# Residual in chunk stacks at the norms between the layers' halves, normed in place by wide operations

## The chip, the cores and the metric

One core of a Trainium2 chip runs the whole kernel. The metric is the device time in microseconds (us); lower is better. TensorE does the matrix products; VectorE, ScalarE and GpSimd do elementwise work on tiles in SBUF (VectorE and ScalarE also in PSUM, where the products land); SP issues nearly all transfers. In the profile they are PE, DVE, ACT, POOL and SP.

## What is computed

One inference step of a two-layer decoder trunk in fp32: 1024 prompt tokens and 8 decoded tokens, width 1024, hidden width 2816. Layer 0 mixes with a gated linear recurrence (HGRN2), layer 1 with sliding-window attention on keys and values that are projected once, after layer 0. Every sub-layer adds a gated result to the residual stream `h`, and reads it through an RMS norm with a scale and a shift that come from the conditioning vector (adaLN):

```python
def rms_norm(x, g):
    y = x32 * lax.rsqrt(jnp.mean(x32 * x32, axis=-1, keepdims=True) + EPS)
    return y * g.astype(jnp.float32)
def modulate(x, g, shift, scale):
    return rms_norm(x, g) * (1.0 + scale[:, None, :]) + shift[:, None, :]
...
        h = h + g1[:, None, :] * mix                      # mix = mixer(xn) @ w_o
        xn = modulate(h, norm_w[l, 1], sh2, sc2)
        h = h + g2[:, None, :] * swiglu(xn, w_ffn_in[l], w_ffn_out[l])
        if l == N_A_LAYERS - 1:
            kvn = modulate(h, kv_norm_w, sh_kv, sc_kv)
            k_sh, v_sh = jnp.split(kvn @ w_kv, 2, axis=-1)
```

## The kernel before

**Layout.** Activations lie transposed: features on the 128 partitions (8 tiles, `k` from 0 to 7), the 1032 tokens as columns, the last 8 of them decoded. Two grids cut the columns: `G3` in three chunks of 344 and `G4` in four of 258. The residual is `h[k]`, a tile of 1024 columns for each `k`, with the decoded tokens in `hd`.

**Products.** Each fp32 factor is split in a high and a low part, and `mm3` (L283 to L285) makes three matmuls per block: high x high, high x low, low x high. Weights arrive as raw tiles (SP), ScalarE rounds the high part (L182), and GpSimd subtracts to get the low part (L185, tile `wu`).

**Around the change.** After a mixer its output is multiplied by the output weights in two halves of the contraction: `wo_first` on `G3` (beside the recurrence or the attention of the other heads), `wo_second` on `G4`. Each 128-row block `n` of a chunk takes 12 matmuls (`wo_product`) and ends in `residual` (L718; L722 for the decoded tokens), which adds the gated product to `h`. For each chunk `wo_second` then runs a norm: squares (ScalarE L649, L652) and their sums (L654, on VectorE and GpSimd in turn), the two sums joined (L666), column sums by TensorE (L672), the inverse root by Newton steps of small VectorE operations (L677, L542 to L551), a diagonal matrix of it (L680, "the diagonal" below), a matmul that spreads it over the partitions (L689), a copy to SBUF (L690). `apply_steps` then does three narrow operations per `k`: `h` times scale and norm (VectorE L698), plus the shift, rounded to the high part (ScalarE L702), and the low part (VectorE L703). These steps are generators in the list `later`, of which `step()` advances one at a time between the blocks of the product.

The result feeds the gated product of the feed-forward part, which multiplies 2 x 2 blocks by seven products instead of four times two; `factors` makes the seven right factors from the *split* values, by wide VectorE operations over four `k` (L1255 to L1257 for a difference, L1249 on ScalarE and L1250 on VectorE to split it). `prepare_all` stores `h` to DRAM first (L1294), and `back` loads it again for the second feed-forward product. There the sum of squares (`ToKV` for layer 0) runs in the same way on `G3`; `ToKV` is applied twice, once for keys and values and once for the queries of layer 1. `conditioning` (L472, 128x32 matmuls on the adaLN weights, which SP loads at L276) runs beside `wo_first` and `wo_second` of layer 0.

**The order.** The program is written as these interleaved generators; when the kernel is built, a scheduler fixes the sequence of each engine's instructions, and semaphores tie them. A change of what is written moves rows on every queue. SP's queue is in order too: a store that waits for its data holds the loads behind it.

## Time and profile before

| | |
|---|---|
| median of 3 runs | 2569.52 us (2567.04 to 2572.01) |
| profiled execution, its own time | 2565.16 us |
| its span, first to last instruction | 2563.4 us |
| mean granted TensorE clock | 0.987 |
| busy: TensorE, VectorE, ScalarE, GpSimd | 97%, 56%, 33%, 31% |
| moved by DMA | 293.42 MB, 114 GB/s |

The span is one profiled execution. In timelines the first number is the start in us from the start of the span, the second the busy time, and what stands in square brackets is idle time just before and what ended it. In lists of waits, "A <- B: 6.8, 1, 6.8" says that A's engine sat idle 6.8 us until B let A go, once. The granted clock is a share of full speed.

### The profile page before, as it was taken

The page shows a single profiled execution, that of the slowest core. Times are in us where ns is not written, and L with a number is a line of the kernel's source. Part 1 is how long each engine was busy: PE and PEld are TensorE (multiplying, and loading weights), DVE is VectorE, ACT ScalarE, POOL GpSimd, SP SyncE. Part 2 cuts the span into 40 slices and gives each one's busy share as a digit, 9 for nine tenths or more (in the row PEclk, how much of TensorE's full clock was granted, in tenths as well). Part 3 has the DMA queues.
Part 4 walks back from the last instruction along what each step waited for, and adds up shares of the span by engine and source line. Part 5 has one row for each costly group of instructions (what it writes and reads, how often), then busy time and mean ns, then how long its engine had stood idle before and what let it go on. Part 6 is the DMA issues. An engine that isn't in the chain of part 4 may idle for free.

```text
span 2563.4 us, 52144 instructions
## 1 busy us (share of the span) xinstructions
PE 2478.8 (97%) x21387; PEld 2352.9 (92%) x21387; DVE 1445.2 (56%) x3305; ACT 848.6 (33%) x1952; POOL 805.2 (31%) x602
## 2 busy tenths in 40 slices
PE   7999999999999999999999899999899999999998
PEld 5998999997889999999999898778899999999998
DVE  5545545464687554655433754566985555554336
ACT  4322323231343332332211344554433333323212
POOL 2211121120324443544432231203244444434321
PEclk9999999999999999999999999999999999999999
DMA  9555222239932224225421312332212222254201
GB/s 321 181 187 164 71 68 68 68 92 301 310 124 83 75 77 126 85 84 196 149 75 49 99 46 66 116 125 83 99 59 84 90 76 75 75 190 166 83 26 67
DMA packets 301538, 293.42 MB, mean 114 GB/s; under 512 B 28970, under 2 KB 272571, under 8 KB 301267
## 3 DMA queue, kind: packets, MB, share of 16 engines
q1 hardware_dynamic: 300896, 289.86, 34.6%
q8 instruction: 168, 2.75, 0.4%
q14 instruction: 72, 0.58, 0.1%
q10 hardware_dynamic: 402, 0.22, 0.0%
HBM read 231.27 MB, written 63.99 MB: 115 GB/s over the span
## 4 chain that ended last, share of the span: by engine, by line
PE 84%; DVE 8%; DMA 3%; issue 2%; POOL 1%; ACT 1%; SPq 1%; DVEq 0%; ACTq 0%; POOLq 0%
PE mm L283 19%; PE mm L285 18%; PE mm L284 18%; PE ax L283 6%; PE ax L284 6%; PE ax L285 6%; PE ax L472 2%; PE ax L1656 1%; PE ax L1727 1%; PE ax L917 1%; PE ax L1713 1%; POOL wu L185 1%; DMA c<-in_w_ada_dram 1%; DVE w L698 1%; DVE c L943 1%
## 5 line engine op out<-in xcount | busy, mean ns | idle before, releaser
L185 POOL TENSOR_TENSOR wu<-raw,wu 128x512 fp32r<-128x512 f32 x460 | 631.7, 1381 | 1378.7 <-ACT wu L182 1222.6
L283 PE MATMUL mm<-c,wu 128*128 128x344 f32 (+1 forms) x2032 | 661.7, 327 | 8.4 <-ACT c L702 4.2
L284 PE MATMUL mm<-c,wu 128*128 128x344 f32 (+1 forms) x2032 | 651.8, 321 | 3.7 <-POOL c L1389 2.9
L285 PE MATMUL mm<-c,wu 128*128 128x344 f32 (+1 forms) x2032 | 650.9, 320 | 2.0 <-POOL wu L185 1.2
L182 ACT CAST wu<-raw 128x512 fp32r<-128x512 f32 x460 | 282.7, 620 | 595.2 <-PE mm L285 280.5
L283 PE MATMUL mm<-xq,wu 128*128 128x258 f32 x1448 | 411.9, 284 | 9.5 <-DVE c L1310 5.2
L285 PE MATMUL mm<-xq,wu 128*128 128x258 f32 x1448 | 409.5, 283 | 0.8 <-POOL wu L185 0.8
L284 PE MATMUL mm<-xq,wu 128*128 128x258 f32 x1448 | 409.9, 283 | 0.0
L283 PEld LDWEIGHTS mm<-c,wu 128*128 128x128 f32 x2032 | 385.5, 190 | 25.8 <-issue 12.0
L284 PEld LDWEIGHTS mm<-c,wu 128*128 128x128 f32 x2032 | 386.7, 190 | 9.4 <-issue 3.6
L285 PEld LDWEIGHTS mm<-c,wu 128*128 128x128 f32 x2032 | 386.3, 190 | 4.3 <-issue 2.8
L718 DVE SCALAR_TENSOR_TENSOR c<-mm,ada,c 128x344 f32<-128x344 f32 (+3 forms) x344 | 192.0, 562 | 293.0 <-PE mm L285 292.6
L284 PE MATMUL ax<-xq,wu 128*128 128x258 f32 x1064 | 300.7, 283 | 0.0
L283 PE MATMUL ax<-xq,wu 128*128 128x258 f32 x1064 | 300.6, 283 | 0.0
L285 PE MATMUL ax<-xq,wu 128*128 128x258 f32 x1064 | 300.5, 282 | 0.0
L283 PEld LDWEIGHTS mm<-xq,wu 128*128 128x128 f32 x1448 | 274.1, 189 | 11.5 <-DVE c L1310 6.2
L284 PEld LDWEIGHTS mm<-xq,wu 128*128 128x128 f32 x1448 | 275.5, 190 | 0.2
L285 PEld LDWEIGHTS mm<-xq,wu 128*128 128x128 f32 x1448 | 274.5, 190 | 1.1 <-POOL wu L185 1.1
L284 PEld LDWEIGHTS ax<-xq,wu 128*128 128x128 f32 x1064 | 201.7, 190 | 0.0
L283 PEld LDWEIGHTS ax<-xq,wu 128*128 128x128 f32 x1064 | 201.6, 189 | 0.0
L285 PEld LDWEIGHTS ax<-xq,wu 128*128 128x128 f32 x1064 | 201.0, 189 | 0.0
L938 DVE TENSOR_TENSOR c<-c,c 128x512 f32<-128x512 f32 x56 | 47.1, 841 | 96.7 <-PE ax L917 76.5
(313 smaller groups left out, 3618.1 us busy)
## 6 DMA issues: line engine op xcount, KB each, us to landing
c<-in_w_ada_dram SPq DMA_DIRECT2D x96, 512.0 KB
raw<-in_w_ffn_in_dram SPq DMA_DIRECT2D x152, 256.0 KB
ff<-c SPq DMA_DIRECT2D x44, 516.0 KB
c<-ff SPq DMA_DIRECT2D x44, 516.0 KB
raw<-in_w_ffn_out_dram SPq DMA_DIRECT2D x44, 512.0 KB
raw<-in_w_in_a_dram SPq DMA_DIRECT2D x32, 512.0 KB
out_dram<-c SPq DMA_DIRECT2D x16, 512.0 KB
c<-in_w_ada_kv_dram SPq DMA_DIRECT2D x16, 512.0 KB
```

Of the source, the lines that this page charges most:

```text
L182: i = act.copy(u[:, 0, :], src)
L185: eng.tensor_tensor(u[:, 1, :], src, u[:, 0, :], op=ALU.subtract)
L283: pe.matmul(ps, wh, xh, start=first, stop=False)
L284: pe.matmul(ps, wh, xl, start=False, stop=False)
L285: pe.matmul(ps, wl, xh, start=False, stop=last)
L472: pe.matmul(ada_ps[q][32 * j : 32 * j + 32, 256 * i : 256 * i + 256], cT[:, k, :], u[i][:, j, :], start=(k == 0 and i == 0), stop=(k == KT ...
L698: dve.scalar_tensor_tensor(t, h[k][:, s], modA[:, m, k, 0:1], self.R[:, s], op0=ALU.mult, op1=ALU.mult)
L718: dve.scalar_tensor_tensor(hc, ps[:, : g.pl[c]], ada[:, gate + n, 0:1], hc, op0=ALU.mult, op1=ALU.add)
L917: pe.matmul(ps[32 * j : 32 * j + 32, c * 32 : (c + 1) * 32], KS[:, t0 : t0 + 32], QP[:, t0 : t0 + 32], start=True, stop=True, tile_positio ...
L938: dve.tensor_tensor(q4[:, :, 1, :], q4[:, :, 1, :], bc(p3[:, :, 0], 2, M), op=ALU.mult)
L943: dve.tensor_tensor(nxt, p3[:, :, 0], p3[:, :, 1], op=ALU.mult)
L1656: pe.matmul(psv[hf][:, gi, s0:256], q[2 * gp + gi][r, tb * P : (tb + 1) * P], kT[a][r, (tb - 1) * P + s0 : (tb + 1) * P], start=True, stop ...
```

## The change

- The residual is held by chunk: a `Stack` on a grid has for each chunk tiles of four `k` x 258 columns (`G4`) or three `k` x 344 (`G3`), loaded by `reload_stack`. `residual` writes into it. For that, `wo_first` runs on `G4` as `wo_second` does.
- `StackNorm` squares several `k` at a time, and norms the chunk in place: one multiplication of the stack by the norm (L807), eight ScalarE operations with scale and shift (L827), one wide copy for the high part (L831), one wide subtraction for the low part (L835). Each chunk is stored to DRAM before that (`st.move`, L659), in place of the eight stores later on.
- `factors` takes its differences from the unsplit, normed stacks: one operation each (L1391).
- `ToKV` is a `StackNorm` on `G3`; its second application needs no multiplication by the norm any more.

Lines that only moved have other numbers in the changed kernel: L472 is L473, L689 is L727, L718 is L842, L1310 is L1440.

```diff
+    class Stack:
+        def __init__(self, g):
+            self.g, self.m = g, TOK // g.w
+            self.t = [{} for _ in range(g.n)]
+        def rows(self, i):
+            return slice(i * self.m, min(KT, (i + 1) * self.m))
+        def groups(self):
+            return range(-(-KT // self.m))
+        def part(self, c, i, n):
+            r = self.rows(i)
+            return self.t[c][i][:, : r.stop - r.start, :n]
+        def at(self, k, g, c):
+            return self.t[c][k // self.m][:, k % self.m, : g.pl[c]]
+        def move(self, dram, cs, load):
+            for c in cs:
+                n, s = self.g.pl[c], self.g.prompt(c)
+                for i in self.groups():
+                    d = dram[self.rows(i)][:, :, s].rearrange("k p n -> p k n")
+                    if load:
+                        self.t[c][i] = p4.tile([P, self.m, self.g.w], F32, tag="c4", name=nm("hs"))
+                        sp.dma_start(self.part(c, i, n), d)
+                    else:
+                        sp.dma_start(d, self.part(c, i, n))
...
-            dve.tensor_tensor(self.acc[0][:, s], self.acc[0][:, s], self.acc[1][:, s], op=ALU.add)
+            self.merge(c)
             for _ in range(3):
                 yield LAG
             ps = axp()
             for j in range(n):
-                c0 = g.cs[c] + j * Q
-                pe.matmul(
-                    ps[:Q, j : j + 1], self.acc[0][:, c0 : c0 + Q], ones[:, 0:1], start=True, stop=True
-                )
+                pe.matmul(ps[:Q, j : j + 1], self.sums(c, j), ones[:, 0:1], start=True, stop=True)
...
+    class StackNorm(Norm):
+        def __init__(self, st):
+            self.g, self.st = st.g, st
+            self.acc = {}
+            self.R = big()
+            self.b = 2 if st.m == 4 else 3
+        def accs(self, c):
+            if self.b == 3:
+                if c not in self.acc:
+                    self.acc[c] = p4.tile([P, 3, W], F32, tag="c4", name=nm("sq"))
+                return self.acc[c]
+            if c // 2 not in self.acc:
+                self.acc[c // 2] = p4.tile([P, 4, self.g.w], F32, tag="c4", name=nm("sq"))
+            return self.acc[c // 2][:, 2 * (c % 2) : 2 * (c % 2) + 2, :]
+        def square(self, c, k):
+            b, m, n = self.b, self.st.m, self.g.pl[c]
+            if k % b < b - 1 and k < KT - 1:
+                return
+            k0 = k - k % b
+            src = self.st.t[c][k0 // m][:, k0 % m : k0 % m + k - k0 + 1, :n]
+            dst = self.accs(c)[:, : k - k0 + 1, :n]
+            if k0 == 0:
+                act.activation(dst, src, AF.Square)
+            else:
+                t = p4.tile([P, b, self.g.w], F32, tag="c4", name=nm("sq"))[:, : k - k0 + 1, :n]
+                act.activation(t, src, AF.Square)
+                eng = pool if (b == 2 and k0 == 4) else dve
+                eng.tensor_tensor(dst, dst, t, op=ALU.add)
...
+        def merge(self, c):
+            n, a = self.g.pl[c], self.accs(c)
+            for i in range(1, self.b):
+                dve.tensor_tensor(a[:, 0, :n], a[:, 0, :n], a[:, i, :n], op=ALU.add)
+        def sums(self, c, j):
+            return self.accs(c)[:, 0, j * Q : j * Q + Q]
+        def scale_rows(self, c, i):
+            t = self.st.part(c, i, self.g.pl[c])
+            R = self.R[:, self.g.prompt(c)]
+            dve.tensor_tensor(t, t, bc(R, 1, t.shape[1]), op=ALU.mult)
+        def apply_steps(self, c, m, x, first=True, keep=False):
+            sh = MODS[m][0]
+            n, w = self.g.pl[c], self.g.w
+            if c == self.g.last:
+                td = small([P, KT, NB], "ntd", 1)
+                dve.tensor_tensor(td, hd, bc(self.R[:, T:TOK], 1, KT), op=ALU.mult)
+                dve.tensor_tensor(td, td, modA[:, m, :, 1:9], op=ALU.mult)
+                dve.tensor_tensor(td, td, ada[:, sh : sh + KT, 1:9], op=ALU.add)
+            for i in self.st.groups():
+                r = self.st.rows(i)
+                nk = r.stop - r.start
+                if first:
+                    self.scale_rows(c, i)
+                t = self.st.t[c][i]
+                f = p4.tile([P, self.st.m, w], F32, tag="c4", name=nm("xf")) if keep else t
+                for k in range(nk):
+                    kk = r.start + k
+                    act.activation(
+                        f[:, k, :n], t[:, k, :n], AF.Identity, scale=modA[:, m, kk, 0:1], bias=ada[:, sh + kk, 0:1]
+                    )
+                if n < w:
+                    dve.tensor_copy(f[:, :nk, n:], td[:, r, :])
+                yield 1
+                xh, xl = (z[:, :nk, :] for z in x.q[c][i])
+                act.copy(xh, f[:, :nk, :])
+                dve.tensor_tensor(xl, f[:, :nk, :], xh, op=ALU.subtract)
+                if i == self.st.groups()[-1]:
+                    x.ready.add(c)
+                yield 1
...
     def residual(ps, c, n, gate, tdec, g=G3):
-        hc = h[n][:, g.prompt(c)]
+        hc = res[-1].at(n, g, c)
...
-    def wo_first(o, gate, before_last=None):
+    def wo_first(o, gate, before_last=None, g=G4):
         tdec = small([P, KT, NB], "tdec", 2)
         us = [ws.next() for _ in range(4)]
-        for c in range(NCH):
-            if c == LAST and before_last:
+        for c in range(g.n):
+            if c == g.last and before_last:
                 before_last()
             for n in range(KT):
-                wo_product(us[n // 2], o, c, n, gate, tdec)
+                wo_product(us[n // 2], o, c, n, gate, tdec, g)
                 if n % 2:
                     yield
...
-    def wo_second(o, gate, m, beside=iter(())):
+    def wo_second(o, gate, m, back, beside=iter(())):
         tdec = small([P, KT, NB], "tdec", 2)
         us = [ws.next() for _ in range(4)]
-        N = Norm(G4)
+        st = res[-1]
+        N = StackNorm(st)
         x = Quads()
         def then(c):
+            st.move(back, [c], False)
             yield from N.finish(c)
             yield LAG
             yield from N.apply_steps(c, m, x)
...
-        return x
-    def reload_h(src, *cs):
+        return x, st
...
+    def reload_stack(src, g):
+        st = Stack(g)
+        res.append(st)
+        st.move(src, [0], True)
+        yield
+        st.move(src, range(1, g.n), True)
...
         def part(raw):
             xh, xl = quad()
-            act.copy(flat(xh), raw)
-            dve.tensor_tensor(flat(xl), raw, flat(xh), op=ALU.subtract)
+            act.copy(xh, raw)
+            dve.tensor_tensor(xl, raw, xh, op=ALU.subtract)
             return xh, xl
-        def diff(p, q):
-            t, e = big(), big()
-            dve.tensor_tensor(t, flat(p[0]), flat(q[0]), op=ALU.subtract)
-            dve.tensor_tensor(e, flat(p[1]), flat(q[1]), op=ALU.subtract)
-            dve.tensor_tensor(t, t, e, op=ALU.add)
-            return t
+        def diff(p, q, dst):
+            dve.tensor_tensor(flat(dst), flat(p), flat(q), op=ALU.subtract)
+            return dst
         def steps():
+            t2 = []
             for i in range(2):
-                b11, b12, b22 = x[2 * i][0], x[2 * i + 1][0], x[2 * i + 1][1]
-                t1 = diff(b12, b11)
+                b11, b12, b22 = f[2 * i][0], f[2 * i + 1][0], f[2 * i + 1][1]
+                t1 = diff(b12, b11, b11)
                 yield
                 xs7[i][5] = part(t1)
                 yield
-                dve.tensor_tensor(t1, flat(b22[0]), t1, op=ALU.subtract)
-                dve.tensor_tensor(t1, t1, flat(b22[1]), op=ALU.add)
+                t2.append(diff(b22, t1, t1))
                 yield
-                xs7[i][6] = part(t1)
+                xs7[i][6] = part(t2[i])
                 yield
             for i in range(2):
-                t3 = diff(x[2 * i + 1][1], x[2 * i + 1][0])
+                t3 = diff(f[2 * i + 1][1], f[2 * i + 1][0], f[2 * i + 1][0])
                 yield
                 xs7[i][7] = part(t3)
                 yield
             for i in range(2):
-                t4 = diff(x[2 * i][1], xs7[i][6])
+                t4 = diff(f[2 * i][1], t2[i], t2[i])
                 yield
                 xs7[i][4] = part(t4)
                 yield
...
         def prepare_all():
-            for k in range(KT):
-                sp.dma_start(hs[k], h[k])
-            yield 1
...
-    reload_h(xs, 0)
-    reload_h(xs, 1, 2)
-    run((wo_first(o, 16), 12), (hgrn_tail, 28), (conditioning((4, 5), (4,)), 12))
+    for _ in reload_stack(xs, G4):
+        pass
+    run((wo_first(o, 16), 16), (hgrn_tail, 28), (conditioning((4, 5), (4,)), 12))
     o = mixed(osc, 1)
     mixed_dec(o, odec, 1)
-    X = wo_second(o, 16, 1, conditioning((6, 3), (2, 3)))
-    class ToKV(Norm):
+    back = [dp.tile([KT, P, T], F32, name=f"hs{i}") for i in range(2)]
+    X, st = wo_second(o, 16, 1, back[0], conditioning((6, 3), (2, 3)))
+    hsc = dp.tile([KT, P, T], F32, name="hsc")
...
+    class ToKV(StackNorm):
         def then(self, c):
+            self.st.move(hsc, [c], False)
             yield from self.finish(c)
             yield LAG
-            yield from self.apply_steps(c, 2, self.x)
+            yield from self.apply_steps(c, 2, self.x, keep=True)
...
-    hsc = dp.tile([KT, P, T], F32, name="hsc")
-    for k in range(KT):
-        sp.dma_start(hsc[k], h[k])
...
-        later.append([nkv.apply_steps(c, 3, X), False])
+        later.append([nkv.apply_steps(c, 3, X, first=False), False])
...
-    reload_h(hsc, 0)
+    loads = reload_stack(hsc, G4)
+    next(loads)
...
-    run((wo_first(o, 64, dec_first), 12), (second, 24), (dec, 20))
+    run((wo_first(o, 64, dec_first), 16), (second, 24), (dec, 20))
     o = mixed(asc, 1)
     mixed_dec(o, adec, 1)
-    X = wo_second(o, 64, 4)
+    X, st = wo_second(o, 64, 4, back[1])
```

What the build then orders differs in many places; three of them follow.

SP, layer 0, at the start of `wo_second` (raw: the weights of the feed-forward part; c<-in_w_ada_kv_dram: the conditioning's weights). Before:

```order
L195 DMA raw_7684<-in_w_ffn_in_dram 128x8x128
L195 DMA raw_7692<-in_w_ffn_in_dram 128x8x128
L276 DMA c_900_7867<-in_w_ada_kv_dram 128x4x256
L276 DMA c_901_7869<-in_w_ada_kv_dram 128x4x256
L276 DMA c_903_7880<-in_w_ada_kv_dram 128x4x256
L276 DMA c_904_7882<-in_w_ada_kv_dram 128x4x256
```

Now (hs_7771 is the copy of the residual in DRAM, hs_6576 and hs_6578 the stacks of chunk 0):

```order
L195 DMA raw_7790<-in_w_ffn_in_dram 128x8x128
L195 DMA raw_7798<-in_w_ffn_in_dram 128x8x128
L659 DMA hs_7771<-hs_6576 128x4x258
L659 DMA hs_7771<-hs_6578 128x4x258
L276 DMA c_904_7963<-in_w_ada_kv_dram 128x4x256
L276 DMA c_905_7965<-in_w_ada_kv_dram 128x4x256
```

The two stores of chunk 0 stand between the raw weights and the twelve loads of the conditioning.

TensorE, layer 0, in `wo_second` (ax_7871 and ax_7967: the conditioning's sums; mm and ax else: the output product). Before:

```order
L285 MATMUL ax_7986<-c_839_7609,wu_6630 128x258
L472 MATMUL ax_7871<-c_913_7945,cT 32x256 x4
L472 MATMUL ax_7871<-c_914_7947,cT 32x256 x4
L472 MATMUL ax_7871<-c_915_7957,cT 32x256 x4
L472 MATMUL ax_7871<-c_916_7959,cT 32x256 x4
L283 MATMUL mm_8027<-c_833_7603,wu_6627 128x258
```

Now:

```order
L285 MATMUL mm_8117<-c_843_7709,wu_6619 128x258
L473 MATMUL ax_7967<-c_916_8038,cT 32x256 x4
L283 MATMUL mm_8117<-c_845_7711,wu_6622 128x258
L284 MATMUL mm_8117<-c_846_7712,wu_6622 128x258
L285 MATMUL mm_8117<-c_845_7711,wu_6622 128x258
L283 MATMUL mm_8117<-c_847_7713,wu_6622 128x258
L284 MATMUL mm_8117<-c_848_7714,wu_6622 128x258
L285 MATMUL mm_8117<-c_847_7713,wu_6622 128x258
L283 MATMUL ax_8134<-c_841_7707,wu_7776 128x258
L284 MATMUL ax_8134<-c_842_7708,wu_7776 128x258
L285 MATMUL ax_8134<-c_841_7707,wu_7776 128x258
L473 MATMUL ax_7967<-c_917_8040,cT 32x256 x4
```

The conditioning's tiles, four in one run before, stand singly between nine matmuls of the product.

VectorE, layer 0's KV norm, from the end of chunk 1's product on (c_1589 to c_1596: the residual; xt: the split values). Before:

```order
L718 SCALAR_TENSOR_TENSOR c_1589_13921<-ax_16321,ada,c_1589_13921 128x336
L722 TENSOR_TENSOR tdec_15989<-ax_16321,ada 128x8
L698 SCALAR_TENSOR_TENSOR w_16337<-c_1591_13925,modA,c_1845_15946 128x344
L698 SCALAR_TENSOR_TENSOR w_16341<-c_1592_13927,modA,c_1845_15946 128x344
L718 SCALAR_TENSOR_TENSOR c_1590_13923<-mm_16345,ada,c_1590_13923 128x336
L703 SCALAR_TENSOR_TENSOR xt_15948<-w_16337,ada,xt_15947 128x344
L703 SCALAR_TENSOR_TENSOR xt_15950<-w_16341,ada,xt_15949 128x344
L722 TENSOR_TENSOR tdec_15989<-mm_16345,ada 128x8
L698 SCALAR_TENSOR_TENSOR w_16361<-c_1593_13929,modA,c_1845_15946 128x344
L698 SCALAR_TENSOR_TENSOR w_16365<-c_1594_13931,modA,c_1845_15946 128x344
L718 SCALAR_TENSOR_TENSOR c_1591_13925<-ax_16369,ada,c_1591_13925 128x336
L703 SCALAR_TENSOR_TENSOR xt_15950<-w_16361,ada,xt_15949 128x344
```

Now (hs_13886 to hs_13898: stacks of the residual, sq: sums of squares, c_1796: the norm):

```order
L807 TENSOR_TENSOR hs_13886<-hs_13886,c_1796_15903 128x1032
L842 SCALAR_TENSOR_TENSOR hs_13896<-mm_16232,ada,hs_13896 128x344
L807 TENSOR_TENSOR hs_13888<-hs_13888,c_1796_15903 128x1032
L786 TENSOR_TENSOR sq_16146<-sq_16146,sq_16246 128x688
L842 SCALAR_TENSOR_TENSOR hs_13898<-ax_16259,ada,hs_13898 128x336
L799 TENSOR_TENSOR sq_16146<-sq_16146 128x344
L846 TENSOR_TENSOR tdec_15946<-ax_16259,ada 128x8
L799 TENSOR_TENSOR sq_16146<-sq_16146 128x344
L842 SCALAR_TENSOR_TENSOR hs_13898<-mm_16276,ada,hs_13898 128x336
L846 TENSOR_TENSOR tdec_15946<-mm_16276,ada 128x8
L807 TENSOR_TENSOR hs_13890<-hs_13890,c_1796_15903 128x688
L835 TENSOR_TENSOR xt_15905<-xf_16250,xt_15904 128x1032
```

The narrow pairs L698 and L703 are gone; wide scalings (L807), sums (L786, L799) and a subtraction (L835) stand between the residuals.

## Rows read from the trace of the kernel before

**Rows 1.** Page, part 1: busy us (share of span), instructions

```profile
PE 2478.8 (97%) x21387; PEld 2352.9 (92%) x21387; DVE 1445.2 (56%) x3305; ACT 848.6 (33%) x1952; POOL 805.2 (31%) x602
```

**Rows 2.** TensorE's waits: line <- releaser: us in total, times, longest

```profile
PE ax L689 <- DVE tdec L722: 6.8, 1, 6.8
PE ax L689 <- DVE w L680: 6.4, 2, 3.6
...
PE mm L283 <- DVE c L1310: 5.2, 3, 2.3
...
PE ax L1503 <- ACT c L1490: 3.5, 1, 3.5
...
PE mm L283 <- DVE tdec L722: 3.2, 1, 3.2
```

**Rows 3.** Windows, TensorE: us, busy (xcount), granted clock, DMA share, GB/s

```profile
725.70:731.70 6.00, 5.93 (x36) 0.73 0.56 175
1454.20:1460.20 6.00, 5.98 (x21) 0.57 1.13 282
1507.70:1513.70 6.00, 5.84 (x22) 0.50 0.88 212
1831.60:1837.60 6.00, 5.91 (x35) 0.73 0.83 336
1909.40:1915.40 6.00, 5.91 (x36) 0.72 0.23 92
```

**Rows 4.** Windows, two plain stretches: length, PE, PEld, DVE, ACT, POOL busy, clock, DMA

```profile
880.00:900.00 20.00, 20.00 (x169) 20.00 (x169) 11.02 (x22) 6.33 (x14) 9.15 (x7) 1.00 0.25 81
1260.00:1280.00 20.00, 20.00 (x129) 20.00 (x128) 10.10 (x19) 7.37 (x9) 9.86 (x6) 1.00 0.30 108
```

**Rows 5.** Timeline of TensorE (start us, us, ...): four conditioning tiles, then one

```profile
669.34 0.28 PE L285 MATMUL ax<-c,wu 128*128 128x258 f32 x1
669.55 1.93 PE L472 MATMUL ax<-c,cT 128*32 128x256 f32 x32
671.41 0.39 PE L283 MATMUL mm<-c,wu 128*128 128x258 f32 x1
...
704.27 0.39 PE L283 MATMUL mm<-c,wu 128*128 128x258 f32 x1
704.58 0.64 PE L472 MATMUL ax<-c,cT 128*32 128x256 f32 x8
705.15 0.39 PE L284 MATMUL mm<-c,wu 128*128 128x258 f32 x1
```

**Rows 6.** Timeline of SP (twelve loads) and VectorE (chunk 0's last residual), layer 0

```profile
661.41 15.12 SPq L276 DMA_DIRECT2D c<-in_w_ada_kv_dram  x12
...
668.22 0.49 DVE L718 SCALAR_TENSOR_TENSOR c<-mm,ada,c 128x258 f32<-128x258 f32 x1 [0.89 <-PE mm L285]
```

**Rows 7.** Groups by line and shape, VectorE: xcount | busy us, mean ns

```profile
L1250 DVE TENSOR_TENSOR xq<-c,xq 128x1032 fp32r<-128x1032 f32 x16 | 19.7, 1230 | 10.0 <-ACT xq L1249 10.0
```

**Rows 8.** Timeline of VectorE, two wide differences in the gated product, layer 0

```profile
803.50 2.31 DVE L1255 TENSOR_TENSOR c<-xq,xq 128x1032 f32<-128x1032 f32 x1
805.74 2.29 DVE L1256 TENSOR_TENSOR c<-xq,xq 128x1032 f32<-128x1032 f32 x1
```

**Rows 9.** Timeline of GpSimd and of ScalarE, KV norm

```profile
1490.46 10.76 POOL L185 TENSOR_TENSOR wu<-raw,wu 128x512 fp32r<-128x512 f32 x1 [36.76 <-ACT wu L182]
...
1506.74 0.62 ACT L182 CAST wu<-raw 128x512 fp32r<-128x512 f32 x1 [6.72 <-DMA raw<-in_w_q_b_dram]
```

**Rows 10.** Timeline of VectorE, KV norm: a residual, and chunk 1's diagonal

```profile
1430.37 0.58 DVE L718 SCALAR_TENSOR_TENSOR c<-mm,ada,c 128x344 f32<-128x344 f32 x1 [1.89 <-PE mm L285]
...
1453.13 0.94 DVE L680 TENSOR_TENSOR w<-ident,ny 86x344 f32<-86x344 f32 x1
```

**Rows 11.** Timeline of VectorE, layer 1: chunk 2's last residual and its diagonal

```profile
1808.10 0.49 DVE L718 SCALAR_TENSOR_TENSOR c<-mm,ada,c 128x258 f32<-128x258 f32 x1 [0.31 <-PE mm L285]
...
1831.21 0.42 DVE L680 TENSOR_TENSOR w<-ident,ny 86x258 f32<-86x258 f32 x1
```

47 lines of the change are left out of this document (33 added, 14 removed).

## The prediction

> **What bounds the kernel now.** I read the page first. TensorE is busy 97% of the span [rows 1], so work taken off VectorE, ScalarE or GpSimd shortens nothing unless TensorE waits for it. Next I read TensorE's waits, by what ended them [rows 2]: the reader should pick the ones that end on VectorE or ScalarE in stages that the change touches. Those are 6.8 us and 6.4 us for the broadcast matmul of the norm (L689), 5.2 us for a PSUM bank that L1310 frees, 3.5 us for ScalarE's copy L1490, and 3.2 us for L722, together 25.1 us. Third, the granted clock just behind five of these waits, in stretches of 6 us [rows 3]: 0.73, 0.57, 0.50, 0.73 and 0.72 of full speed, the engine having stood idle before each. The missing shares of 6 us are 1.6, 2.6, 3.0, 1.6 and 1.7 us, 10.5 us in all. So at most 25.1 + 10.5 = 35.6 us of this run can be won; all else is matmul.
>
> The sum is made against the profiled execution, 2565.2 us, which is 4.3 us below the median of the three runs, 2569.5; I shift the result by that. A difference under 0.2%, 5.1 us, counts as no change, about what a measurement here can tell.
>
> **What it adds on TensorE.** (1) The first half of the output product goes from chunks of 344 columns to 258. Two plain stretches give the pace [rows 4]: 169 matmuls in 20 us, 118.3 ns, at 258 columns, and 129, 155.0 ns, at 344. Per layer 384 x 118.3 = 45.4 us replace 288 x 155.0 = 44.6 us: **+1.6 us** for both layers.
>
> (2) The order lists show the conditioning matmuls (L472; 128x32 instead of 128x128) scattered in single tiles between other matmuls where they stood in fours; over the program 45 runs of them become 55. The timeline prices it [rows 5]: with four tiles in one run, 669.34 to 671.41 passes between the starts of the matmuls around them, 2.07 us less one step of 0.12, so 1.95 us. A single tile takes 704.27 to 705.15, less 0.12: 0.76 us. Four singles cost 3.04, so each extra run (3.04 - 1.95) / 3 = 0.36 us, and ten cost **+3.6 us**. Nothing hides this, it is TensorE's own time.
>
> (3) Layer 0's store of the normed residual now stands on SP's queue ahead of twelve loads for the conditioning. Before, SP issued these from 661.41 on, 1.26 us apart [rows 6]. Its two stores need chunk 0's last residual, which ended at 668.22 + 0.49 = 668.7 [rows 6], so the loads start 7.3 us later, behind two stores of their own size. The first tile lands at 668.7 + 4 x 1.26 = 673.7 at the earliest, and its flight after that; by the order TensorE wants it 24 matmuls behind the run of four that starts at 669.55 [rows 5], at 669.55 + 1.95 + 24 x 0.118 = 674.3. The bounds are 0 and, if TensorE takes over the whole delay, 7.3 + 2 x 1.26 = 9.8. I take **+1.5 us**, near the lower, since 673.7 is so near 674.3 and single tiles are then asked for more slowly (0.76 + 9 x 0.118 = 1.8 us apart) than they were issued. The later stores stand behind loads that are issued by then, and the stores that leave the end of the half were behind everything urgent: nothing. In layer 1 and for the stores of the KV norm, the rows behind are loads of weights used much later: nothing, 0 to 2.
>
> **What it takes away.** (4) The factors lose 14 of 30 wide operations per layer, each about 1.23 us [rows 7]. They are off the path except where two in a row, each stretched to 2.31 us beside GpSimd [rows 8], stand ahead of L1310, for whose bank TensorE waits. One difference now takes one operation, not three: I take the whole 5.2 us of L1310 [rows 2] and the slow clock behind it, 1.7: **-6.9 us**, bounds 0 and -6.9.
>
> (5) In the KV norm VectorE ran an unbroken stream of half-microsecond operations with two SBUF inputs (L698, L703). A weight addition of GpSimd that began at 1490.46 beside it took 10.76 us, the next raw weights were therefore asked for late, and ScalarE sat 6.72 us for them with L1490 behind it [rows 9]. The stream is replaced by three scalings or copies and three subtractions a chunk. I keep 1.2 of the 3.5 us and drop the slow clock: -2.3 - 3.0 = **-5.3 us**, bounds 0 and -6.5. ScalarE pays: eight narrow operations as before plus three wide copies a chunk, which I bound by VectorE's 1.23 at that width: up to 9 x 1.23 = 11 us over some 60. I count them at nothing, hidden in ScalarE's idle time there, of which the 6.72 are the largest piece; without that cover L1490 is late again.
>
> (6) The wait of 6.8 us at the KV norm's chunk 1: VectorE was busy without a break from 1430.37 to the diagonal at 1453.13 + 0.94 [rows 10], 23.7 us. Its own work in that I count from the order: 18 narrow two-input operations and nine residuals at about 0.5 us (0.58 by the row, less the overlap with the next), and some 3 us of small ones, 16.5; the rest is stretching beside GpSimd. By the new order the same nine residuals (4.5), the small ones (3.0), four wide operations at 1.15 (1.23 less the overlap: 4.6) and some 1.3 us of narrower adds stand there, 13.4 us; and three narrow GpSimd additions leave, worth 3 x 0.44 = 1.3 by the stretch of the diagonal there (0.94 against 0.5). So it comes 3.1 + 1.3 = 4.4 us earlier. But L689's successor, L727, now stands 20 matmuls, 3.1 us, earlier on TensorE, which so meets it sooner. Net **-1.3 us** with the clock as before; bounds -9.4 (6.8 + 2.6) and +3.
>
> (7) The second half of the output product: the apply drops from sixteen narrow VectorE operations per chunk, up to 0.49 each by the residual of that width [rows 6], to two scalings and two subtractions: 7.8 to 4 x 1.23 = 4.9 us. But the order pulls two wide factor differences ahead of the diagonal of chunk 2. In layer 1, from chunk 2's last residual to the end of that diagonal, 1808.10 to 1831.63 passed [rows 11], 23.5 us; eight weight additions stretched 8 x 1.1 = 8.8 of it (2.31 - 1.23, [rows 7, 8]), so 14.7 was VectorE's own. Now six wide operations (6 x 1.15 = 6.9), four narrower (2.0), eight residuals (8 x 0.5 = 4.0) and Newton's steps (1.4) stand there, 14.3, beside the same additions. So I leave the waits of 6.4 and 3.2 us and their two slow stretches: **0**, bounds -12.8 and +5.
>
> Sum: 1.6 + 3.6 + 1.5 - 6.9 - 5.3 - 1.3 + 0 = -6.8, so 2558.4 for the profiled run and **2562.7 us** for the median.
>
> **A rule that speaks against it.** Beside a wide operation, GpSimd and VectorE stretch each other: 2.31 us against 1.23 alone [rows 7, 8], and GpSimd 10.76 beside a stream of short ones [rows 9]. The Trainium skill, "SBUF — State Buffer", section "Who interferes with whom", says that a VectorE instruction with two SBUF inputs and a GpSimd instruction that reads SBUF exclude each other for the whole instruction, whichever was first. By that rule, longer VectorE instructions hold each weight addition off longer; the trace agrees that one waits out the other, and shows that an unbroken stream of short ones holds GpSimd off longest.
>
> **Rivals.** *All waits go.* VectorE's load falls enough that the diagonals are never late and the clock never drops: -35.6 + 1.6 + 3.6 + 1.5 = -28.9, so 2540.6. For it: VectorE was full in just those places. Against it: my counts for (6) and (7) show hardly less work ahead of the diagonals. 0.20.
>
> *The change doesn't reach the path.* The diagonals and L1490 stay late, for the work ahead of them is only packed into wider pieces; only (4) comes: 1.6 + 3.6 + 1.5 - 6.9 = -0.2, so 2569. 0.15.
>
> *GpSimd starves (slower).* Wide scalings and subtractions stand ahead of the weight additions in the last half of each output product, and each of the eight per layer starts up to one wide operation, 1.15 us, late: 2 x 8 x 1.15 = 18.4 us, 2562.7 + 18.4 = 2581. It decides from the point where the gated product's first weights come after TensorE has reached them. For it: [rows 9]. Against: none of the waits of [rows 2] ends on a weight addition. 0.15.
>
> *The loads are late (3).* At its bound of 9.8, and with a slow clock of 1.6 behind it: -6.8 + 8.3 + 1.6 = +3.1, so 2573. 0.05.
>
> **How the numbers follow.** My forecast has 0.45; its own range, from half of (4) and (5) failing to half of (6) and (7) coming, is 2553 to 2569, on both sides of 2564.4, where faster begins: 0.27 faster and 0.18 the same. All waits gone adds 0.20 to faster; not reaching the path 0.03 faster, 0.08 same, 0.04 slower (over 2574.7); late loads 0.02 and 0.03; starvation 0.15 slower. That makes 0.52, 0.29 and 0.19. The range takes in the forecast, the upper half of the first rival and the lower part of starvation: 2543 to 2577.
>
> **What would show it.** TensorE's instructions: 16229 rows in its order against 16041, the conditioning tiles at about 0.76 us each where single. Its waits: L1440 (was L1310) near 0, L727 still 12 or so in all, L1503's successor near 1. No GpSimd addition over 4 us in the KV norm. SP: the twelve loads from about 669 on. I am wrong if L727's waits vanish, if new waits on weights (POOL wu) show after the output products, or if ScalarE's wide copies end TensorE's waits in the KV norm.

## The result and the profile after

The changed kernel takes **2548.74 us** in the median of four runs (2547.05 to 2554.92), the kernel before 2568.28 in four runs beside it: a ratio of 0.9926, 95% interval 0.9906 to 0.9947. That is faster, by about 19 us; the forecast was 2562.7, some 7 us faster than the median of the kernel before that was known then, with a range of 2543 to 2577. The profiled execution took 2554.92 us (span 2553.1), the one before 2565.16.

The page of the changed kernel, part 1 (against [rows 1]):

```profile
PE 2481.1 (97%) x21579; PEld 2355.2 (92%) x21579; DVE 1370.6 (54%) x3117; ACT 877.9 (34%) x1929; POOL 777.0 (30%) x577
```

VectorE is busy 75 us less, ScalarE 29 us more, TensorE 2 us more with 192 more matmuls. None of that is the gain. It lies in TensorE's waits and in the clock behind them. The waits (line <- releaser: us in total, times, longest):

```profile
PE ax L727 <- DVE w L718: 9.8, 4, 6.1
...
PE mm L283 <- ACT c L1518: 5.4, 2, 4.5
...
PE mm L283 <- DVE hs L842: 2.3, 2, 1.7
```

Against [rows 2], the waits that end on L1310 (now L1440) and on L1490 are gone, and the 6.8 us in the KV norm (the norm of chunk 1 between layer 0's second product and the keys and values) are 1.4:

```profile
1446.49 0.82 PE L727 MATMUL ax<-w,ones 86*128 86x344 f32 x2 [1.40 <-DVE w L718]
```

The 6.1 that is left stands in layer 1's `wo_second`, where 3.6 (L680) and 3.2 (L722) stood. New is L842, a residual that waits for a reload. The granted clock behind the waits (length; TensorE, its weight loads, VectorE, ScalarE, GpSimd busy; clock; DMA share), against [rows 3]:

```profile
729.80:735.80 6.00, 6.00 (x54) 4.30 (x55) 4.70 (x7) 4.34 (x8) 0.21 (x1) 1.00 0.64 176
1446.50:1452.50 6.00, 6.00 (x37) 5.80 (x38) 6.00 (x11) 4.60 (x8) 2.87 (x1) 1.00 0.65 161
1496.00:1502.00 6.00, 5.95 (x45) 5.59 (x44) 1.10 (x2) 2.92 (x6) 2.36 (x2) 1.00 0.65 153
1821.30:1827.30 6.00, 6.00 (x26) 5.82 (x27) 3.93 (x8) 5.33 (x10) 0.95 (x1) 0.51 0.25 85
1899.00:1905.00 6.00, 6.00 (x52) 6.00 (x51) 2.87 (x7) 1.24 (x2) 2.82 (x3) 1.00 0.00 0
```

Four of the five slow stretches run at full clock; the fourth, behind the 6.1 us of standing still, is slower than before (0.51 against 0.73).

To place the gain I cut each trace at the same matmul (the n-th that has an operand of a given name) and averaged three executions of each kernel, the first profile and two more of each that come below. In us:

| stretch of TensorE's work | before | changed | difference | forecast |
|---|---|---|---|---|
| start to layer 0's output product (code that the change leaves alone) | 565.1 | 565.4 | +0.3 | 0 |
| layer 0's output product | 187.4 | 188.4 | +1.0 | +5.9 |
| first fifth of its gated product (factors) | 71.3 | 67.7 | -3.5 | -6.9 for both layers |
| rest of the gated product | 364.3 | 365.9 | +1.6 | 0 |
| second product, KV norm, keys, values, queries, attention's first half | 471.5 | 456.8 | -14.7 | -6.6 |
| layer 1's output product | 193.0 | 197.1 | +4.0 | +0.8 |
| its gated product (factors) | 434.6 | 430.1 | -4.5 | see above |
| to the end | 276.3 | 277.4 | +1.1 | 0 |

The sum is -14.7, as the three spans give it (2548.8 against 2563.5); the timed medians differ by 17 to 20. The first row, the same code in all, lies between 559.7 and 569.2 in the thirteen profiles of this study: whole executions can differ by 9.5 us for that alone, and a stretch is the better witness. Of the +1.6 us in the rest of the gated product, 1.5 come at one place, at about 1010 us, and only in two of the three executions: TensorE waits 1.0 and 0.8 us there in both kernels, but behind that the granted clock is 0.83 over 10 us in those two and 1.00 in the third and in the kernel before. Whether the clock falls behind the same short waits can thus differ from one execution to the next.

### The profile page after: what moved, and what is told of

It reads as the page before. It is cut to its first block, busy times and chain, and to the rows that moved or that the text cites. A ratio compares the mean times of both kernels' runs of the same rounds, so it can differ in the third digit from the quotient of the medians.

```text
span 2553.1 us, 52217 instructions
## 1 busy us (share of the span) xinstructions
PE 2481.1 (97%) x21579; PEld 2355.2 (92%) x21579; DVE 1370.6 (54%) x3117; ACT 877.9 (34%) x1929; POOL 777.0 (30%) x577
## 4 chain that ended last, share of the span: by engine, by line
PE 88%; DVE 5%; DMA 4%; issue 2%; SPq 1%; POOL 1%; ACT 0%; DVEq 0%; POOLq 0%
PE mm L283 20%; PE mm L285 19%; PE mm L284 19%; PE ax L283 6%; PE ax L285 6%; PE ax L284 6%; PE ax L473 2%; PE ax L1790 1%; PE ax L1861 1%; DMA c<-in_w_ada_dram 1%; PE ax L1847 1%; PE ax L1041 1%; DVE c L1067 1%; DMA c<-ff 1%; PE ax L1130 1%
## 5 line engine op out<-in xcount | busy, mean ns | idle before, releaser
L185 POOL TENSOR_TENSOR wu<-raw,wu 128x512 fp32r<-128x512 f32 x460 | 618.4, 1351 | 1303.2 <-ACT wu L182 1111.2
L283 PE MATMUL mm<-c,wu 128*128 128x344 f32 (+1 forms) x2096 | 675.0, 323 | 11.9 <-ACT c L1518 5.4
L284 PE MATMUL mm<-c,wu 128*128 128x344 f32 (+1 forms) x2096 | 664.1, 317 | 3.1 <-POOL c L1519 2.0
L285 PE MATMUL mm<-c,wu 128*128 128x344 f32 (+1 forms) x2096 | 663.8, 317 | 0.0
L283 PEld LDWEIGHTS mm<-c,wu 128*128 128x128 f32 x2096 | 399.6, 191 | 26.7 <-issue 10.2
L284 PEld LDWEIGHTS mm<-c,wu 128*128 128x128 f32 x2096 | 400.9, 191 | 8.1 <-POOL c L1519 2.8
L285 PEld LDWEIGHTS mm<-c,wu 128*128 128x128 f32 x2096 | 400.2, 191 | 4.6 <-issue 4.5
L842 DVE SCALAR_TENSOR_TENSOR hs<-mm,ada,hs 128x344 f32<-128x344 f32 (+3 forms) x228 | 120.3, 533 | 180.1 <-PE mm L285 166.0
L285 PEld LDWEIGHTS ax<-xq,wu 128*128 128x128 f32 x1064 | 200.9, 189 | 0.0
L842 DVE SCALAR_TENSOR_TENSOR c<-mm,ada,c 128x344 f32<-128x344 f32 (+1 forms) x132 | 75.1, 572 | 117.1 <-PE mm L285 116.3
```

The lines of the kernel that those rows point to most:

```text
L185: eng.tensor_tensor(u[:, 1, :], src, u[:, 0, :], op=ALU.subtract)
L283: pe.matmul(ps, wh, xh, start=first, stop=False)
L284: pe.matmul(ps, wh, xl, start=False, stop=False)
L285: pe.matmul(ps, wl, xh, start=False, stop=last)
L842: dve.scalar_tensor_tensor(hc, ps[:, : g.pl[c]], ada[:, gate + n, 0:1], hc, op0=ALU.mult, op1=ALU.add)
```

## The experiments

### The changed kernel again

No edit.

> The changed kernel as it is, traced and timed once more. Its four executions so far lie between 2547.1 and 2554.9 us, and the profiled one is the slowest. Theory A (one transfer varies): the profiled one lost some 6 us at 2300 us, where TensorE waited 4.5 us for activations read back from DRAM (c<-ff) and then ran at half clock; a new trace shows less than 2 us there, and a time of 2547 to 2550. Rival B (the loss belongs to the change): the wait of over 4 us is there again, and the time is near 2554.

> The changed kernel as it is, once more, on the same chip as the two kernels with early loads. Theory A: 0.9915 to 0.9940 of the kernel before, with TensorE's wait of about 2 us behind the residual's DMA in layer 1's wo_first in its trace. Rival B: on another chip the wait is not there, and the time is that of the kernel with early loads.

Measured: 2547.23 us in six runs (0.9928, 0.9915 to 0.9941), and on another chip 2549.59 in six (0.9936, 0.9923 to 0.9948). The 4.5 us wait behind L1518, seen in the first profile, is 1.1 and 3.7 here: a transfer that varies. The wait behind the residual's reload is there in both, 1.7 and 3.0 us. Theory A holds in both.

### The kernel before, two more profiles

No edit.

> The kernel before, traced once more. Up to the end of the first stage (520 us) both kernels run the same instructions in the same order; the traces so far reach the matmul behind the sixth head at 520.3 us (before) and 523.0, 516.6, 518.0, 515.0 and 516.7 us (five traces of the changed kernel and its variants). Theory A (that stage varies by itself): this trace lies between 515 and 523, and may be earlier than 518. Rival B (the change also shortens this stage, by what lies where in SBUF or DRAM): it lies at 519 or later, as before.

> The kernel before, a third trace, for the same question: theory A between 515 and 523, rival B 519 or later. In both, the waits that the change touches are those of the first trace within 0.5 us: 6.8 for chunk 1's diagonal of the KV norm, 5.2 for L1310, 3.5 for L1490.

Measured: 2561.18 and 2569.5 us. Of the 8.3 us between them 3.8 lie in the first stretch of the table, 1.9 in layer 0's output product, 1.5 in its factors and 1.1 at the end; the other stretches agree within 0.3. So the waits are the kernel's own, and the largest part of the spread of whole executions is the first stretch's. It takes 562.5 and 566.3 us here and 563.1 to 569.2 in the three executions of the changed kernel: the change does not shorten it, as theory A has it.

### Factors from the split values again

```diff
-        def diff(p, q, dst):
-            dve.tensor_tensor(flat(dst), flat(p), flat(q), op=ALU.subtract)
-            return dst
+        def diff(p, q):
+            t, e = big(), big()
+            dve.tensor_tensor(t, flat(p[0]), flat(q[0]), op=ALU.subtract)
+            dve.tensor_tensor(e, flat(p[1]), flat(q[1]), op=ALU.subtract)
+            dve.tensor_tensor(t, t, e, op=ALU.add)
+            return t
```

> Only the factors are put back: differences from the split values, 30 wide VectorE operations per layer instead of 16. Theory A (the forecast's term 4): TensorE waits again for the banks that L1310 frees (L1440 in the changed kernel), in both layers, 5.2 us and a slow clock of 1.7: 7 to 9 us slower than the changed kernel. Rival B (those waits went with the lighter queue, not with the factors): within 2 us of the changed kernel.

Measured: 2555.15 us (0.9957, 0.9944 to 0.9969), 7.9 above the changed kernel on the same chip. Layer 0's factors take 70.65 us again and layer 1's 434.24: both close to the values of before. The wait is back (TensorE's waits of this kernel, L1443 being L1440 there):

```profile
PE mm L283 <- DVE c L1443: 3.7, 4, 1.6
```

So term (4) is the factors' own, and worth 7.1 us by these two stretches (2.9 and 4.2), 7.9 by the times; theory A holds.

### The KV norm as it was

`ToKV` goes back to the narrow `Norm` on `G3`, with both applications complete, and with it the residual in rows that this norm needs: `reload_h` in place of `reload_stack`, and the eight stores behind the norm. All else stays.

```diff
-    class ToKV(StackNorm):
+    class ToKV(Norm):
...
-        later.append([nkv.apply_steps(c, 3, X, first=False), False])
+        later.append([nkv.apply_steps(c, 3, X), False])
```

> Only the KV norm is put back: narrow operations on a residual in rows, stores of the residual behind it. The rest is as in the changed kernel. Theory A (the trace's ledger): the late diagonal of chunk 1 (7.2 us and a slow clock) and the late L1490 (3.8 us and a slow clock) come back, 13 to 16 us slower than the changed kernel. Rival B (the forecast's sizes, terms 5 and 6): 6 to 7 us slower. Rival C (the relief came from elsewhere): within 2 us.

Measured: 2562.11 us (0.9987, 0.9978 to 0.9997, twelve runs), 14.9 above the changed kernel. The fifth stretch takes 470.2 us, and both waits stand there again:

```profile
PE ax L727 <- DVE tdec L846: 6.9, 1, 6.9
...
PE ax L1643 <- ACT c L1630: 3.3, 1, 3.3
```

GpSimd in that kernel, at the place of [rows 9] (start, busy, count):

```profile
1483.64 19.37 POOL L185 TENSOR_TENSOR wu<-raw,wu 128x512 fp32r<-128x512 f32 x8 [36.77 <-ACT wu L182]
```

The first of these eight took 10.76 us, as in [rows 9]; the others 1.26 to 1.30. The KV norm, with its residual's form, is worth 13 to 15 us (theory A), twice what I gave it; the rival there, the forecast's own 6 to 7, falls.

### The KV norm's wide operations cut into narrow ones

The scaling and the last subtraction run per `k` at 344 columns, in the KV norm only. The work is the same, the instructions are shorter and more.

```diff
+            if self.b == 3:
+                for k in range(t.shape[1]):
+                    dve.tensor_tensor(t[:, k, :], t[:, k, :], R, op=ALU.mult)
+                return
...
+                if self.b == 3:
+                    for k in range(nk):
+                        dve.tensor_tensor(xl[:, k, :], f[:, k, :], xh[:, k, :], op=ALU.subtract)
```

> The changed kernel with the scalings and the low-part subtractions of the KV norm cut into operations of 344 columns, over the same elements and in the same places. Theory A (the gain there is in work that VectorE no longer has: the second scaling, the scale and shift that went to ScalarE, the fewer residuals ahead of the diagonal): within 3 us of the changed kernel, no GpSimd addition over 4 us but the one that stands in both. Rival B (the width itself did it, as short operations in a row hold GpSimd off): GpSimd additions of 5 us and more return, with a wait of 2 us or more for L1490's successor (L1630) or the diagonal, 4 to 9 us slower.

Measured: 2550.69 us (0.995, 0.9937 to 0.9963). Inside the fifth stretch three pieces can be told apart (in us; first profile and two more of before; three of the changed kernel; the others one each):

| piece | before | changed | flat KV norm | narrow |
|---|---|---|---|---|
| to 21 matmuls into the first product on the KV norm | 271.3 | 261.8 | 270.6 | 265.0 |
| of this, from the 1501st of the 1584 matmuls of the second feed-forward product on | 26.9 | 19.3 | 27.2 | 22.7 |
| the next 42 | 7.3 | 8.5 | 7.4 | 7.3 |
| where L1490 was late | 22.4 | 15.9 | 21.2 | 15.9 |

GpSimd's additions where [rows 9] showed 10.76 us, in the narrow kernel (two of eight) and then in the changed one:

```profile
1486.76 1.37 POOL L185 TENSOR_TENSOR wu<-raw,wu 128x512 fp32r<-128x512 f32 x1 [0.16 <-ACT wu L182]
1488.59 1.49 POOL L185 TENSOR_TENSOR wu<-raw,wu 128x512 fp32r<-128x512 f32 x1 [0.46 <-ACT wu L182]
```

```profile
1484.54 1.30 POOL L185 TENSOR_TENSOR wu<-raw,wu 128x512 fp32r<-128x512 f32 x1 [29.52 <-ACT wu L182]
1486.58 1.52 POOL L185 TENSOR_TENSOR wu<-raw,wu 128x512 fp32r<-128x512 f32 x1 [0.73 <-ACT wu L182]
1488.40 3.19 POOL L185 TENSOR_TENSOR wu<-raw,wu 128x512 fp32r<-128x512 f32 x2 [0.30 <-ACT wu L182]
```

And VectorE of the narrow kernel just before and beside it:

```profile
1479.26 3.74 DVE L841 TENSOR_TENSOR xt<-hs,xt 128x344 fp32r<-128x344 f32 x8 [0.57 <-ACT xt L838]
1483.82 1.61 DVE L841 TENSOR_TENSOR xt<-hs,xt 128x344 fp32r<-128x344 f32 x3 [0.82 <-ACT xt L838]
1486.20 2.73 DVE L841 TENSOR_TENSOR xt<-hs,xt 128x344 fp32r<-128x344 f32 x3 [0.77 <-ACT xt L838]
```

Narrow instructions alone do not starve GpSimd: beside the last group here it is VectorE that is stretched (2.73 us for three, 1.61 for the three before), and the additions take 1.4 and 1.5. What else differs from [rows 9]: the multiplication is gone from the second application, and the subtractions come in threes and eights with VectorE idle in between, since each group waits for ScalarE. Which of these two frees GpSimd no run separates; no addition was asked for at the start of the stream of eight.

The first piece is 9.5 us shorter in the changed kernel, but only 7.6 of that lie at the KV norm. The rest comes earlier, where the second product starts: TensorE waits 2.1 to 2.6 us there for the copies of what is read back from DRAM (L1388) in the kernel before and 1.0 to 1.5 in the changed one, and one of the three executions of before ran at a lower clock behind it. Whether the change shortens these waits no run shows. The narrow kernel loses 3.3 of the 7.6, with TensorE's wait for the diagonal at 3.1 us instead of 1.4:

```profile
PE ax L727 <- DVE w L718: 3.1, 1, 3.1
```

This is the order as much as the width: three of the narrow subtractions (1.36 us) stand just ahead of the diagonal there, where the wide one stands behind it in the changed kernel. At the second piece the narrow kernel gains 1.2. By its ratio it is 4 to 6 us slower than the changed kernel, which would speak against theory A's 3 us, but the intervals overlap, and its fifth stretch (458.4 us) is only 1.6 longer; its span, 2548.5, is that of the changed kernel's three. So the time does not decide between the theories. Rival B's sign, additions of 5 us and more, did not come.

### The first half of the output product on 258 columns, alone

The kernel before, with `wo_first` on `G4` and nothing else of the change.

```diff
-    def wo_first(o, gate, before_last=None):
+    def wo_first(o, gate, before_last=None, g=G4):
...
-    run((wo_first(o, 64, dec_first), 12), (second, 24), (dec, 20))
+    run((wo_first(o, 64, dec_first), 16), (second, 24), (dec, 20))
```

> The kernel before with only the first half of the output product on chunks of 258 columns, in both layers. The order list has the conditioning's tiles in 44 runs here (45 before, 55 in the changed kernel). Theory A (the forecast's term 1, matmul time): 1.6 us slower than the kernel before. Rival B (its narrower residuals and other interleaving cost or save waits as well): over 4 us away from it on either side.

Measured: 2572.52 us (1.0027, 1.0014 to 1.004), some 7 us slower than before and not the 1.6 of theory A, nearly all in layer 1's output product: 200.9 us instead of 193.0. SP's queue there (start, time over the group, count):

```profile
1673.01 4.88 SPq L1562 DMA_DIRECT2D c<-nd  x4
1677.94 3.85 SPq L1235 DMA_DIRECT2D c<-hsc  x8
```

and TensorE behind it:

```profile
1680.00:1690.00 10.00, 10.00 (x43) 7.78 (x42) 4.10 (x25) 4.56 (x20) 0.00 (x0) 0.50 0.92 313
1690.00:1700.00 10.00, 9.99 (x52) 7.24 (x53) 5.73 (x31) 5.19 (x17) 0.00 (x0) 0.70 0.01 2
```

In the kernel before, the reload of the residual's other chunks is issued at nearly the same time (1678.18), but chunk 0's last residual starts only at 1675.30. Here it starts at 1670.72: a chunk of 258 is done sooner, and VectorE then does nothing for ten us. TensorE's gaps from 1676.15 on (0.9 and 0.7 us) carry other names in its list of waits, "issue" (the profile shows nothing that was waited for) and a copy of ScalarE; half clock follows them. The reading is that the product cannot go on before the reload, which stands behind loads of the decode (L1562), and that TensorE is left with what little the decode has. Two runs further down test it on the changed kernel.

### The reload issued early

The changed kernel, with all loads of layer 1's second residual issued at once, ahead of the attention's second half.

```diff
-    loads = reload_stack(hsc, G4)
-    next(loads)
+    for _ in reload_stack(hsc, G4):
+        pass
```

> The changed kernel, with all eight loads of layer 1's second residual half issued on SyncE's queue right behind those of its first chunk, ahead of the attention's second half and with it ahead of the decode's cache and decode-vector loads. Theory A: the reload of chunk 1 is late because it stands behind the decode's loads, which wait for round trips, while the first chunk of 258's wo_first now ends some 3.5 us sooner. Then the wait of 2.0 us behind the residual's DMA, and the clock of about 0.78 behind it, go; layer 1's wo_first takes 112 to 113 us instead of 114.4 to 115.1, and the kernel takes 0.9906 to 0.9920 of the kernel before, 2 to 4 us less than the changed kernel. Rival B: the loads that are brought forward push the decode's cache loads back, the decode or the second half of the attention starts later, and TensorE gains nothing there or loses 1 to 5 us: 0.9925 or more.

Measured: 2547.01 us (0.9922, 0.9906 to 0.9938), beside 2549.59 for the changed kernel run along with it: the intervals overlap. First VectorE of that changed kernel, TensorE's wait for it and TensorE's windows; then the wait and the windows in the kernel with early loads:

```profile
1653.66 0.49 DVE L842 SCALAR_TENSOR_TENSOR hs<-mm,ada,hs 128x258 f32<-128x258 f32 x1 [0.96 <-PE mm L285]
1664.76 1.67 DVE L842 SCALAR_TENSOR_TENSOR hs<-mm,ada,hs 128x258 f32<-128x258 f32 x4 [10.62 <-DMA hs<-hsc]
```

```profile
PE mm L283 <- DVE hs L842: 3.0, 1, 3.0
...
1662.00:1672.00 10.00, 6.98 (x37) 6.74 (x35) 3.72 (x14) 2.25 (x9) 0.00 (x0) 0.66 1.04 332
1672.00:1682.00 10.00, 10.00 (x74) 8.09 (x74) 7.01 (x37) 6.11 (x24) 0.00 (x0) 1.00 0.18 35
```

```profile
PE mm L283 <- DVE hs L842: 0.6, 1, 0.6
...
1662.00:1672.00 10.00, 10.00 (x87) 9.81 (x87) 2.92 (x6) 0.59 (x1) 0.00 (x0) 1.00 0.58 177
1672.00:1682.00 10.00, 10.00 (x62) 8.20 (x61) 6.96 (x40) 5.44 (x24) 0.00 (x0) 0.85 0.15 40
```

The late reload is shown: with it brought forward, the wait falls from 3.0 to 0.6 us and that window runs at full clock. But the clock falls in the next ten us instead (0.85), and layer 1's first half keeps 113.9 us, against 114.4 to 117.0 with the wait and 111.9 before. Theory A's mechanism holds; its size does not: it wanted 112 to 113 us there, the trace shows a gain of 0.5 to 3, and in the time none is resolved.

### The factors behind the second diagonal

Each factor difference keeps its place in the written order, so that none is pulled ahead of chunk 2's diagonal.

```diff
-            dve.tensor_tensor(flat(dst), flat(p), flat(q), op=ALU.subtract)
+            i = dve.tensor_tensor(flat(dst), flat(p), flat(q), op=ALU.subtract)
+            tc.keep_in_program_order(i)
```

> The changed kernel with the factor differences held behind what is written before them on VectorE's queue, so that none stands ahead of the diagonal of chunk 2 in either layer. Theory A (term 7: the two differences there hold the diagonal back): TensorE's wait for the diagonal falls from 6.1 us in layer 1 by 2.4 to 3.6, and from 1.4 us in layer 0 to nothing; 4 to 8 us faster with what the clock gives back. Rival B (GpSimd's eight weight additions in one unbroken stretch of 13.4 us hold it back, by stretching Newton's steps): the wait stays over 4.5 us, within 2 us of the changed kernel.

Measured: 2547.85 us (0.9924, 0.991 to 0.9938), the changed kernel's time. Layer 1's wait is 4.3 instead of 6.1, a fall of 1.8 where theory A wanted 2.4 to 3.6; layer 0's stays (1.6 us). In the time rival B is right. GpSimd in the changed kernel there, then this kernel's waits and TensorE behind the longest of them:

```profile
1803.36 13.45 POOL L185 TENSOR_TENSOR wu<-raw,wu 128x512 fp32r<-128x512 f32 x8 [4.11 <-ACT wu L182]
```

```profile
PE ax L727 <- DVE w L718: 8.3, 4, 4.3
...
1809.80:1815.80 6.00, 5.87 (x25) 5.72 (x26) 4.25 (x7) 4.11 (x7) 2.65 (x2) 0.50 0.34 110
```

A shorter wait that is still followed by half clock gives little back. In the changed kernel eight weight additions run without a break while Newton's steps stand on VectorE, and L546 and L550 are stretched alike; the third row is a wide operation behind the last of these additions:

```profile
1810.62 1.25 DVE L546 TENSOR_SCALAR ny<-nt 86x3 int32<-86x3 int32 x1
...
1811.91 1.21 DVE L550 SCALAR_TENSOR_TENSOR nt<-ny 86x3 f32<-86x3 f32 x1
...
1818.92 1.22 DVE L835 TENSOR_TENSOR xq<-hs,xq 128x1032 fp32r<-128x1032 f32 x1
```

Undisturbed, the same L550 took 0.15 us at 1817.52. Beside a weight addition, the operation of 3 columns takes as long as the one of 1032 without.

### Both edits together

The early reload and the pinned differences in one kernel.

> The same as the kernel with the early loads, and the differences of layer 1's (and layer 0's) factors kept behind the second diagonal, as in the run that did this alone. Theory A: the two gains add, since they lie in different halves of the output product: TensorE's wait in the second half stays at 4 to 4.5 us, that in the first is gone, and the time is 0.989 to 0.9915 of the kernel before. Rival B: neither gain reaches the time: 0.992 to 0.9935, as the changed kernel.

Measured: 2548.16 us (0.9939, 0.9922 to 0.9957). Its layer 1 output product is the shortest of the changed kernels, 193.8 us against 197.1, but layer 1's factors take 432.4 instead of 430.1 and the KV stretch 458.8. Rival B is nearer: no version here beats the changed kernel by more than can be measured.

## Why the prediction was right on the time and wrong on the places

The time fell in the forecast's direction and in its range, at nearly three times its size, because the terms of the KV norm were too small and two costs in layer 0 did not come. It lies outside what I gave the forecast itself (2553 to 2569), and inside the range only because that takes in the upper half of a rival that is not what happened; to that extent the range held by luck.

**Waits of the KV norm, (6): wrong, the largest miss.** The step that failed is "by the new order the same nine residuals ... stand there". They do not: from chunk 1's last residual to the diagonal stand six, that one included. VectorE in the changed kernel, that residual, one stretched subtraction, the stretched Newton step and the diagonal:

```profile
1431.44 0.57 DVE L842 SCALAR_TENSOR_TENSOR hs<-mm,ada,hs 128x344 f32<-128x344 f32 x1
...
1437.20 2.31 DVE L835 TENSOR_TENSOR xt<-xf,xt 128x1032 fp32r<-128x1032 f32 x1
...
1440.74 1.23 DVE L546 TENSOR_SCALAR ny<-nt 86x4 int32<-86x4 int32 x1
...
1445.83 0.51 DVE L718 TENSOR_TENSOR w<-ident,ny 86x344 f32<-86x344 f32 x1
```

From the residual to the diagonal's end pass 14.9 us, where [rows 10] had 23.7 and I had worked out 19.3. Three residuals follow the diagonal now, which my own order said, and two of the four wide operations have only 688 columns: VectorE's own work is some 10.4 us instead of 13.4, and the five operations that are stretched beside GpSimd lose some 4.5 instead of 5.9 (estimates, from what the same operations take undisturbed in this trace). So TensorE stands 1.4 us instead of 6.8 and then runs at full clock instead of 0.57: 7.6 us less at this place, near my bound of -9.4, not -1.3. Of these the wait gives 5.4; the clock, which I had left as it was, gives about the rest, 2.6 by [rows 3]. It gives 1.2 back at the join of the sums (L799), which TensorE's L712 now meets late.

**L1490, (5): right in kind, cut short in size.** I forecast -5.3 and bounded it at -6.5; the piece gives -6.5. I had kept 1.2 us of the wait for safety, and none is left. ScalarE's wide copies were indeed hidden: none of TensorE's waits in the KV norm ends on them. No GpSimd addition there takes over 3.2 us, as forecast. How GpSimd was held is sharper now. VectorE of the kernel before, beside the addition of 10.76 us, at its start and at the end of the stream:

```profile
1490.63 0.57 DVE L698 SCALAR_TENSOR_TENSOR w<-c,modA,c 128x344 f32<-128x344 f32 x1
...
1497.93 2.00 DVE L698 SCALAR_TENSOR_TENSOR w<-c,modA,c 128x336 f32<-128x336 f32 x4
1499.85 0.22 DVE L708 TENSOR_TENSOR ntd<-hd,c 128x64 f32<-128x64 f32 x1
```

The stream runs without a pause up to 1499.85, the addition ends at 1501.22, and one alone takes some 1.3: it looks as if it began only when the stream was over. The narrow kernel shows that the width of the instructions is not enough to hold it; that the missing pause is what does is my reading, and no run varied the pauses alone. The Trainium skill, "SBUF — State Buffer", section "Who interferes with whom", gives the lock as held for one instruction, by whichever engine issued first. That fits 2.31 us (L835) and 1.21 us (L550) on VectorE's side, and it leaves open how an addition can be held through twenty instructions.

**Factors, (4): right.** -6.9 forecast, at its own bound; -8.0 by the table, 7.1 and 7.9 by the run that undid them.

**Single conditioning tiles, (2): right per tile, and hidden in part by what else happened.** From the matmul ahead to the second one behind, less two steps, a run of four takes 2.06 us and a single tile 0.77, in the trace of before and in the changed kernel's. In layer 0's output product that +3.6 met a wait shorter by 1.5 and a clock of 1.00 in place of 0.73 (1.6), which I had left as they were; with (1) the stretch comes to +1.0.

**Loads behind the store, (3): too pessimistic.** SP of the changed kernel, against [rows 6]:

```profile
666.87 5.46 SPq L659 DMA_DIRECT2D hs<-hs  x2
672.42 15.10 SPq L276 DMA_DIRECT2D c<-in_w_ada_kv_dram  x12
```

They start 11.0 us later, of which 2.6 are the first stretch of this execution: 8.4, more than the 7.3 that I worked out for the stores ahead of them (9.0 and 10.8 in the two other executions). Still TensorE's waits show next to nothing on them, 0.3 us in one execution of three, instead of +1.5.

**The second half, (7): right in layer 1, wrong in layer 0.** In layer 1 the waits for the diagonals come to 7.1 us where 6.8 stood, as forecast. In layer 0 it goes from 2.8 to 1.3 us (the 6.4 of [rows 2] were 3.6 in layer 1 and this), with the slow clock.

**The first half on 258, (1): the arithmetic right, a queue left out.** In layer 0 it costs about what the pace said. In layer 1 it costs 2.6 to 5.1 us (the first half takes 114.4 to 117.0 instead of 111.9), and 7.1 by itself in the kernel before. I had priced only the matmuls, and looked at SP in layer 0, not in layer 1: the chunk that ends sooner asks for a reload that stands behind the decode's loads. That is the rival "the loads are late", in another place and for other loads.

Of the rivals, "all waits go" was nearest in time (2540.6), but it isn't what happened: 9.8 us on L727 and a stretch at 0.51 are left. Starvation of GpSimd did not come: in the three profiles of the changed kernel 0.8, 0.8 and 1.6 us of waiting end on its additions. "The change doesn't reach the path" is refuted by the run with the KV norm as it was: its two waits are back there, and 13 to 15 us with them.

## What to carry to other kernels

Count what stands ahead of a critical instruction in the new order, one by one: a count carried over from the old order put some 3 us too much ahead of the diagonal here, and with the clock left as it was the term missed by 6. When a tile gets smaller, something ends sooner, so look up on every queue what it asks for next and what that stands behind. And after a wait look at the clock: a wait cut from 6.1 to 4.3 us with half clock behind both bought nothing that could be measured, while the one cut from 6.8 to 1.4 brought the full clock with it. Such a fall of the clock is not certain either: behind the same waits of 1.0 and 0.8 us it came in two executions of three.

## What the runs showed that was not expected

A first stage with the same code throughout takes 559.7 to 569.2 us from execution to execution, nearly twice the 0.2% that a measurement can tell; stretches between equal matmuls, within one trace, resolve a microsecond where whole times do not. A tiny VectorE operation, 86 x 3 elements, takes 1.21 us instead of 0.15 beside a GpSimd weight addition, the same as a wide one takes alone. Newton's steps are a chain of such operations: in layer 1's second half six of them come to 6.8 us instead of some 0.9 beside the eight additions, ahead of a matmul that waits.
